# A hybrid stream step: conv sums later, cached keys turned later, values fetched earlier, samples' sums later, and other places for the last tiles

## The chip, the cores and the metric

The kernel runs on one core of one Trainium2 chip. The metric is the device time of one execution in microseconds (us); lower is better. The engines are named as the profile names them: PE (matrix products), PEld (its weight loads), DVE, ACT, POOL (element-wise work), SP (which here issues DMA transfers).

## The reference

One layer of a hybrid trunk, for 512 prompt frames and 64 sample frames (576 together), model width 2048, float32. Half of the input projection feeds eight heads of stick-breaking attention, the other half a gated convolution of three taps over eight channel groups.

```python
hn = rmsnorm(x, g_norm1)
proj = hn @ w_in
q, k, v, gb, gc, hc = split(proj)                 # 3 x 1024 for attention, 3 x 1024 for the conv
q, k = rmsnorm(q), rmsnorm(k)                     # per head
o_attn = stick_breaking_blocks(q, [k_past, k], [v_past, v])
#   z = q k / sqrt(128); A[t,s] = beta_ts * prod_{s<j<t}(1 - beta_tj), s < t
u = gc * hc
o_conv = gb * (conv_w[0]*u[t-2] + conv_w[1]*u[t-1] + conv_w[2]*u[t])
mix = concat([rmsnorm(o_attn), rmsnorm(o_conv)])  # each over its 1024 channels
x = x + mix @ w_out
h2 = rmsnorm(x, g_norm2)
x = x + (silu(h2 @ w_gate) * (h2 @ w_up)) @ w_down
```

Only the sample frames attend to 512 cached keys and values per head. The outputs are x, the new keys and values token by token, and the conv state.

## The kernel before

Activations lie channel by frame: 128 channels on the partitions, 576 frames in two halves of 288. Every operand is split into a rounded high part and the rest (`hi`, `lo`), and three PE products of them make one float32 product.

**Stage A, the input projection,** goes in units of two 128-column blocks; a unit is computed by seven products (n, p_), p_ from 1 to 7, of 24 matmuls each, after Strassen's scheme. The list `order` gives their order. Units have negative numbers, and −2 (queries and keys of the last pair) and −1 (values) are the last. Partial results go from PSUM to SBUF buffers with tags "ms" and "t" (`kept`), copied by ACT at L429. `a_done` finishes a column block c and half i: for queries and keys it scales, squares, and spawns `normed`, which sums squares over channels on PE (`ss`), forms the root on ACT and DVE, and writes the normed tile E (L794). When both halves are there, E is stored to DRAM and `tokens` transposes it into token order (`tok_a`, `tok_b`). E tiles come from the "e" buffers or, for unit −2, from places in `lpool`. `group_scale` sums the squares of the conv output over channels for both halves (`ssg`, in a PSUM bank of the kind `misc`, of which there are two) and writes the conv's scale. The conv's products `mixc` go through DRAM and are loaded back when `xpool` is released after product (−1,3).

**The first half of the output projection** (`out_proj` over `mixc`) is 32 outputs (`pjo`, one of three PSUM banks `ps_pj`) of eight frames with three matmuls each. DVE scales and adds them to x (L1022, L1023). Interleaved with it run the eight heads, `attend(h)`, one begun every 29 frames. In a head, the scores of key blocks 2, 1, 0 (`z`) are followed by the samples' scores against the cached keys (`zs`); then come the running sums and weights of blocks 2, 1, 0 (the matmuls of `weights`), the values (`po`), the samples' running sums (`sample_weights`, L1128 to L1131) and their values. `keys_cached` transposes the 4 blocks of cached keys on PE (`kc`, a bank of `ps_pj`), copies them with ACT (`kcT`) and issues the load of the next head's keys (`cK`). `load_v` loads new and cached values (`vtok`, `cV`) and splits the new ones.

**What sets the order.** A frame of three matmuls is a tick (about 0.40 us here) of a small event queue, `Pipeline`. What is spawned with a delay, or yields a number, comes back after so many ticks and places its PE instructions at that point. PE's order is thus written by hand. The other engines' orders in these stages come from a planner when the program is built. PSUM banks and buffers are handed on by semaphores: whoever takes one waits for its last reader.

The second half of the output projection and the feed-forward network follow.

Of the kernel before, what the change touches and what calls it, by code (L numbers as in the profile page):

```python
# [10 lines left out]
F32 = mybir.dt.float32  # L11
# [90 lines left out]
def tile_hybrid_stream_step(  # L102
# [320 lines left out]
    def run(n, p_, early=False):  # L423
        st = unit[n]
        kind, fp = UNITS[n][:2]

        def kept(tag):
            t = tmp.tile([P, HALF], F32, tag=tag, name="part", bufs=1)
            nc.scalar.copy(out=t, in_=st["y"])  # L429
            return t  # L430

        def done(c, i, ps, part=None):
            if n < 0:
                a_finish(n, c, i, ps, part)
            elif kind != "down":
                finish(kind, fp, c, i, ps, part)
            elif n in last:
                store_y(n, c, i)

        def add(c, i, ps, part=None):  # L440

            if kind != "down":
                return
            if n in first:
                if part is not None:
                    nc.vector.tensor_tensor(out=acc[fp, c, i], in0=ps, in1=part, op=ALU.add)
                else:
                    nc.scalar.copy(out=acc[fp, c, i], in_=ps)
                return
            if ps is not None:  # L450
                nc.vector.tensor_tensor(out=acc[fp, c, i], in0=ps, in1=acc[fp, c, i], op=ALU.add)
            if part is not None:
                nc.gpsimd.tensor_tensor(out=acc[fp, c, i], in0=acc[fp, c, i], in1=part, op=ALU.add)

        if kind == "down" and p_ == 1 and n in first:
            take_blocks(fp)
        later = kind == "down" and n not in first
        if p_ == 1:
            st["y"] = ps_pj.tile([P, HALF], F32, tag="pj", name="psy")
            multiply(st["y"], n, 1, True)  # L460
            st["p1"] = kept("ms")
        elif p_ == 2:
            x = ps_z.tile([P, 512], F32, tag="z0", name="psx2")[:, :HALF]
            multiply(x, n, 2, True)
            add(0, 0, x, st["p1"])
            done(0, 0, x, st["p1"])
        elif p_ == 6:
            multiply(st["y"], n, 6, False)
            st["u2"] = kept("ms" if n == NGU - 1 else "t")
            if later:  # L470
                add(1, 0, None, st["u2"])
        elif p_ == 7:
            st["w"] = ps_z.tile([P, 512], F32, tag=f"z{n % 2 + 1}", name="psw")[:, :HALF]
            multiply(st["w"], n, 7, True)
            if later:
                add(1, 1, st["w"])
            if "u4" in st:
                done(1, 1, st["w"], st["u4"])
        elif p_ == 5:
            multiply(st["y"], n, 5, False)  # L480
            st["u4"] = kept("acc")
            if early:
                done(0, 1, st["v"], st["u4"])
            if "w" in st:
                add(1, 1, None if later else st["w"], st["u4"])
                done(1, 1, st["w"], st["u4"])
        elif p_ == 3 and early:
            st["v"] = ps_pj.tile([P, HALF], F32, tag="pj", name="psv")
            multiply(st["v"], n, 3, True)
        elif p_ == 3:  # L490
            multiply(st["y"], n, 3, False)
            add(0, 1, st["y"])
            done(0, 1, st["y"])
        else:
            multiply(st["w"], n, 4, False)
            add(1, 0, st["w"], None if later else st["u2"])
            done(1, 0, st["w"], st["u2"])
            del unit[n]
# [284 lines left out]
    def normed(n, h, c, a, b, s2, E):  # L783
        yield 12 if n == -2 else 17
        ms = ss = channel_sums(s2[:, 0], s2[:, 1], a, b, "ss")
        yt = hl_tile("yt")
        y, t = yt[:, :HALF], yt[:, HALF:]
        nc.scalar.activation(out=ms, in_=ss, func=AF.Identity, scale=1.0 / P, bias=epsc)
        nc.scalar.activation(out=y, in_=ms, func=AF.Ln)
        nc.scalar.activation(out=y, in_=y, func=AF.Exp, scale=-0.5)  # L790
        nc.scalar.activation(out=t, in_=y, func=AF.Square)
        nc.vector.scalar_tensor_tensor(out=t, in0=t, scalar=-0.5, in1=ms, op0=ALU.mult, op1=ALU.mult)
        nc.vector.scalar_tensor_tensor(out=t, in0=t, scalar=1.5, in1=y, op0=ALU.add, op1=ALU.mult)
        nc.vector.scalar_tensor_tensor(out=E[:, a:b], in0=E[:, a:b], scalar=col("gk") if c else gqs, in1=t,  # L794
                                       op0=ALU.mult, op1=ALU.mult)
        seen[n, c] = seen.get((n, c), 0) + 1
        if seen[n, c] == 2:
            nc.sync.dma_start(out=qk_dram[h, c], in_=E)
            if c:
                pipe.spawn(tokens(E, kp[:, h, :], ks[:, h, :], None, 5 if n == -2 else 20))  # L800

    def group_scale(acc_, bufs):
        for a, b in HALVES:
# [22 lines left out]
    def a_done(n, c, i, ps, part):  # L826
        kind, g = UNITS[n][:2]
        a, b = HALVES[i]
        if kind in ("v", "qk"):
            if (n, c) not in etile:  # L830
                etile[n, c] = lpool.tile([P, UW - 2], F32, tag=f"c{c}", name="E2")[:, :T] if n == -2 else e_tile(f"E{n}")
            E = etile[n, c]
            bank = ps
            if part is not None:
                nc.vector.tensor_tensor(out=E[:, a:b], in0=ps, in1=part, op=ALU.add)
                ps = E[:, a:b]
            nc.vector.tensor_tensor(out=E[:, a:b], in0=ps, in1=R1[:, a:b], op=ALU.mult)
            if kind == "qk":
                sq = hl_tile("sq")[:, :HALF] if c == i == 1 else bank
                s2 = tmp.tile([P, 2, HALF], F32R, tag="hl", name="s2", bufs=3)  # L840
                nc.scalar.activation(out=sq, in_=E[:, a:b], func=AF.Square)
                nc.scalar.copy(out=s2[:, 0], in_=sq)
                nc.vector.tensor_tensor(out=s2[:, 1], in0=sq, in1=s2[:, 0].bitcast(F32), op=ALU.subtract)
                pipe.spawn(normed(n, g, c, a, b, s2, E))
                return
            seen[n, c] = seen.get((n, c), 0) + 1
            if seen[n, c] == 2:
                h = 2 * g + c
                pipe.spawn(tokens(E, vp[:, h, :], vs[:, h, :], v_dram[h], 3 if n == -1 else 7))
            return  # L850
# [73 lines left out]
             (2 - NA, 5)]  # L924
    for n in range(2 - NA, -3):
        order += [(n + 1, 1), (n, 3), (n, 4), (n + 1, 2), (n + 1, 6), (n + 1, 7), (n + 1, 5)]
    order += [(-2, 1), (-3, 3), (-3, 4), (-2, 2), (-2, 6), (-1, 1), (-2, 5), (-1, 2), (-2, 3), (-2, 7), (-1, 3),
              (-1, 6), (-2, 4), (-1, 5), (-1, 7), (-1, 4)]
    early = {-NA, 1 - NA, -1}
    mixc = []  # L930
# [2 lines left out]
    for k_, (n, p_) in enumerate(order):  # L933
        run(n, p_, n in early)
        if k_ + 4 < len(order):
            prepare(*order[k_ + 4])
            if order[k_ + 4] in ((-2, 3), (-1, 6)):
                load_weight()
        if (n, p_) == (-2, 6):
            pipe.spawn(group_scale(accc[0], 3), 5)  # L940
        if (n, p_) == (-1, 3):
            xpool.release()
            cpool = tc.alloc_tile_pool(name="cpool", bufs=1, reuse_waits="tile", side="right")
            mixc = cpool.tile([P, NG, 2, T], F32R, name="mixc")
            for g in range(NG):
                nc.sync.dma_start(out=mixc[:, g].bitcast(F32), in_=mixc_dram[g])
        if (n, p_) == (-1, 7):
            split_weight(nc.vector)
# [26 lines left out]
    def load_cached_keys(h):  # L975
        nc.sync.dma_start(out=cK, in_=ck[:, h, :].rearrange("(i p) d -> p i d", p=P))

    load_qk(0)
    load_cached_keys(0)
    nc.vector.tensor_scalar(out=neg1r, in0=ident, scalar1=0.0, scalar2=-1.0, op0=ALU.mult, op1=ALU.add)  # L980
    onef = oner.bitcast(F32)
    neg1f = neg1r.bitcast(F32)
# [62 lines left out]
    def open_b():  # L1045
# [6 lines left out]
        v_ = v_.rearrange("p (f i d) -> p f i d", f=2, d=P)  # L1052
        bt["vh"], bt["vl"] = ([v_[:, f, 0], v_[:, f, 1], vz[:, f]] for f in range(2))
        bt["v2"] = v_
        load_v(0)

    def load_v(h):
        nc.sync.dma_start(out=vtok, in_=v_dram[h])
        nc.sync.dma_start(out=cV, in_=cv[:, h, :].rearrange("(i p) d -> p i d", p=P))
        split(bt["v2"][:, 0], bt["v2"][:, 1], vtok[:, 0:2, :])  # L1060
        split(bt["vh"][2], bt["vl"][2], vtok[:, 2, :])

# [11 lines left out]
    def attend(h):  # L1074
# [46 lines left out]
            nc.gpsimd.tensor_tensor(out=sums[:, b * TS : (b + 1) * TS], in0=sums[:, (b + 1) * TS : (b + 2) * TS],  # L1121
                                    in1=sp[:, (b + 1) * TS : (b + 2) * TS], op=ALU.add)
        yield 8
        if h + 1 < NH:
            keys_cached(h + 1)

        def sample_weights():
            mm(zs[:, :320], trir, sph[:, :320], stop=False, **kw)  # L1128
# [25 lines left out]
        behind = weights(1)  # L1154
        with tc.issue_after(behind):
            split(sph, spl, sp)
        yield 4
        mm(zb[0], trir, ph[0], stop=False, **kw)
        mm(zb[0], trir, pl[0], stop=False, **kw)
        mm(zb[0][:, P:], neg1r, s0h, stop=False, **kw)  # L1160
# [15 lines left out]
        for i in (2, 1, 0):  # L1176
            for n, (a_, b_) in enumerate(((vh, ph), (vl, ph), (vh, pl))):
                mm(po[:, i * P : 512], a_[i], b_[i][:, : 512 - i * P], stop=(i == 0 and n == 2), **kw)
            if i == 2:
                yield 1  # L1180
                sample_weights()
                yield 2
            elif i == 1:
                yield 3
        mixed(po, 0, TP)
# [12 lines left out]
            else:  # L1198
                nc.gpsimd.tensor_tensor(out=accA[:, a:b], in0=accA[:, a:b], in1=sq[q], op=ALU.add)
        if h + 1 < NH:  # L1200
            load_v(h + 1)

    PERIOD = 29

# [404 lines left out]
```

## Time and profile before

| | |
|---|---|
| median of 3 runs | 2394.09 us (2393.43 to 2395.15) |
| the profiled execution | 2397.15 us, span 2395.4 us |
| granted PE clock, mean | 0.995 |
| busy share PE, DVE, ACT, POOL | 98%, 81%, 52%, 13% |

The span runs from the first to the last instruction of the profiled execution; its time includes what lies around them. In a timeline, a row is a group of like instructions that follow one another: start, length, engine, line, operation, output and inputs, forms, count, and in brackets the idle time ahead of it with what ended it. Ends of matmuls are modelled.

### The profile page before, as it was taken

What the parts mean: (1) busy time and instruction counts of PE and PEld (TensorE: products, weight loads), DVE (VectorE), ACT (ScalarE), POOL (GpSimd) and SP (SyncE); (2) the same over time, 40 slices, a digit from 0 to 9 for tenths busy, and PEclk for the clock granted to TensorE, in tenths of its full rate; (3) what the DMA queues carried; (4) which work ended last, traced back from release to release, by engine and by line L of the source; (5) the groups of instructions that cost most, each with busy time, mean ns of one, the idle gap of its engine ahead of it and who ended that gap; (6) DMA issues with size and microseconds to landing.
All of it is one profiled execution on the core that took longest, in us unless ns stands there. A gap on an engine that the chain in (4) does not pass through costs nothing.

```text
span 2395.4 us, 43789 instructions
## 1 busy us (share of the span) xinstructions
PE 2350.2 (98%) x17609; PEld 2336.2 (98%) x17609; DVE 1934.0 (81%) x2828; ACT 1234.6 (52%) x2211; POOL 300.3 (13%) x377
## 2 busy tenths in 40 slices
PE   8899999999999999999999999999999899999998
PEld 8899999999899999999999999999999899999998
DVE  7888888787677768888888888888888768887875
ACT  7456656455777545444444444444444444444454
POOL 0111121120233221000000000000000002431211
PEclk9999999999999999999999999999999999999999
DMA  7433343525733333444444444345354936875642
GB/s 254 141 113 104 114 138 89 162 88 188 236 105 104 107 135 106 141 150 132 139 151 142 129 150 153 118 156 159 109 157 139 338 111 212 225 222 194 204 129 79
DMA packets 474900, 360.60 MB, mean 151 GB/s; under 512 B 11278, under 2 KB 460680, under 8 KB 474696
## 3 DMA queue, kind: packets, MB, share of 16 engines
q1 hardware_dynamic: 469528, 351.02, 45.8%
q0 software_dynamic: 5168, 6.79, 1.6%
q8 instruction: 138, 2.26, 0.4%
q14 instruction: 66, 0.54, 0.1%
HBM read 281.39 MB, written 76.37 MB: 149 GB/s over the span
## 4 chain that ended last, share of the span: by engine, by line
PE 82%; DVE 6%; ACT 4%; issue 2%; DMA 1%; POOL 1%; SPq 0%; DVEq 0%; ACTq 0%; POOLq 0%
PE psy L406 43%; PE psw L406 21%; PE psx L406 10%; PE pjo L227 5%; DVE whl L232 1%; DMA v_dram<-tok 1%; PE pw L1391 1%; ACT whl L231 1%; ACT ph L231 0%; PE pot L1514 0%; DVE c L881 0%; ACT whi L179 0%; DMA raw_a<-in_w_down_dram 0%; DVE raw_b L350 0%; DVE wlo L180 0%
## 5 line engine op out<-in xcount | busy, mean ns | idle before, releaser
L232 DVE TENSOR_TENSOR whl<-raw_a,whl 128x1024 fp32r<-128x1024 f32 (+4 forms) x376 | 424.6, 1130 | 70.2 <-ACT whl L231 68.5
L406 PE MATMUL psy<-t,whl 128*128 128x288 f32 x2916 | 437.3, 295 | 0.5 <-ACT part L429 0.5
L231 ACT CAST whl<-raw_a 128x1024 fp32r<-128x1024 f32 (+4 forms) x376 | 352.3, 938 | 141.4 <-PE psx L406 52.1
L406 PE MATMUL psy<-h_s,whl 128*128 128x288 f32 x2724 | 411.8, 295 | 6.8 <-ACT part L429 6.8
L406 PEld LDWEIGHTS psy<-t,whl 128*128 128x128 f32 x2916 | 403.4, 189 | 0.9 <-ACT part L429 0.7
L406 PEld LDWEIGHTS psy<-h_s,whl 128*128 128x128 f32 x2724 | 378.7, 189 | 7.3 <-ACT part L429 7.3
L406 PE MATMUL psw<-t,whl 128*128 128x288 f32 x2592 | 377.2, 295 | 0.0
L406 PEld LDWEIGHTS psw<-t,whl 128*128 128x128 f32 x2592 | 354.0, 189 | 0.2
L232 DVE TENSOR_TENSOR whl<-raw_b,whl 128x1024 fp32r<-128x1024 f32 (+5 forms) x230 | 247.7, 1077 | 89.3 <-ACT whl L231 87.8
L231 ACT CAST whl<-raw_b 128x1024 fp32r<-128x1024 f32 (+5 forms) x230 | 207.2, 903 | 208.2 <-PE psw L406 70.0
L429 ACT COPY part<-psy 128x288 f32<-128x288 f32 x303 | 120.8, 399 | 350.0 <-PE psy L406 345.4
L406 PE MATMUL psx<-h_s,whl 128*128 128x288 f32 x1122 | 166.8, 297 | 2.7 <-DVE gs L1371 2.7
L406 PEld LDWEIGHTS psx<-h_s,whl 128*128 128x128 f32 x1122 | 156.2, 191 | 2.9 <-issue 2.9
L231 ACT CAST whl<-s 128x1024 fp32r<-128x1024 f32 (+5 forms) x101 | 93.3, 924 | 119.9 <-PE psw L406 114.1
L406 PE MATMUL psy<-t12a,whl 128*128 128x288 f32 x1056 | 150.0, 295 | 2.0 <-ACT part L429 2.0
L406 PE MATMUL psw<-t34a,whl 128*128 128x288 f32 x1056 | 150.4, 295 | 1.4 <-DVE ghs L869 0.9
L406 PEld LDWEIGHTS psy<-t12a,whl 128*128 128x128 f32 x1056 | 143.2, 188 | 2.7 <-ACT part L429 2.7
L406 PEld LDWEIGHTS psw<-t34a,whl 128*128 128x128 f32 x1056 | 143.4, 188 | 1.9 <-DVE ghs L869 1.1
L232 DVE TENSOR_TENSOR whl<-s,whl 128x1024 fp32r<-128x1024 f32 (+5 forms) x101 | 107.5, 1065 | 19.9 <-ACT whl L231 18.1
L227 PE MATMUL pjo<-mixc,whi 128*128 128x288 f32 x512 | 119.4, 300 | 0.0
L1334 POOL DMA_DIRECT2D hid_dram<-form x3 | 2.4, 807 | 923.9 <-DVE form L232 923.9
L227 PE MATMUL pjo<-mixa,whi 128*128 128x288 f32 x512 | 102.7, 295 | 0.0
(599 smaller groups left out, 4138.4 us busy)
## 6 DMA issues: line engine op xcount, KB each, us to landing
hid_dram<-form SPq DMA_DIRECT2D x147, 288.0 KB, 2.3
raw_a<-in_w_gate_dram SPq DMA_DIRECT2D x23, 1024.0 KB, 6.4
raw_a<-in_w_up_dram SPq DMA_DIRECT2D x23, 1024.0 KB, 6.0
raw_a<-in_w_in_dram SPq DMA_DIRECT2D x22, 1024.0 KB, 5.5
raw_b<-in_w_in_dram SPq DMA_DIRECT2D x22, 1024.0 KB, 8.2
raw_b<-in_w_gate_dram SPq DMA_DIRECT2D x21, 1024.0 KB, 6.7
raw_b<-in_w_up_dram SPq DMA_DIRECT2D x21, 1024.0 KB, 7.8
h_s<-hid_dram SPq DMA_DIRECT2D x10, 2016.0 KB, 9.9
```

The source lines that it names most:

```text
L227: mm(ps, w_[:, k, csl], x_[:, a:b], start=(k == 0 and n == 0), stop=(k == nk - 1 and n == 2))
L231: cast = nc.scalar.copy(out=hi, in_=src)
L232: (lo_eng or nc.vector).tensor_tensor(out=lo, in0=src, in1=hi.bitcast(F32), op=ALU.subtract)
L406: mm(ps, whl[:, w_, j, :], x_, start=(start and j == 0 and q == 0), stop=(j == len(xs_) - 1 and q == 2), skip_group_check=True)
L429: nc.scalar.copy(out=t, in_=st["y"])
L1334: q.dma_start(out=hid_dram[fp][2 * n - 2 : 2 * n].rearrange("f p t -> p f t"), in_=t.bitcast(F32))
L1391: mm(pss[j, i], w_[:, k, j * P : (j + 1) * P], x_, start=(kk == 0 and k == 0 and n == 0), stop=(kk == 1 and k == 7 and n == 2))
```

## The change

Eight edits, all between about 552 us and the end of the first half of the output projection:

1. `u2` of unit −1 is kept in the buffer "ms" rather than "t".
2. The tokens of unit −2's keys lag 11 ticks rather than 5 behind their norm.
3. Of units −2 and −1 the tiles with c = 0 lie in `lpool`, those with c = 1 in "e" buffers. Before, both of −2 were in `lpool` and both of −1 in "e".
4. Product (−1,3) comes ahead of (−2,7); with it the release of `xpool` and the `mixc` loads.
5. `group_scale` starts 13 ticks after (−2,6) rather than 5.
6. The values of head 0 (`fetch_v`) are requested behind the first queries and keys, and split at tick 15 of head 0; later heads as before.
7. `keys_cached(h + 1)` moves from tick 15 to tick 24 of a head, two ticks behind the second block's weights.
8. `sample_weights` moves from tick 29 to tick 31 of a head.

```diff
-            st["u2"] = kept("ms" if n == NGU - 1 else "t")
+            st["u2"] = kept("ms" if n in (-1, NGU - 1) else "t")
...
-                pipe.spawn(tokens(E, kp[:, h, :], ks[:, h, :], None, 5 if n == -2 else 20))
+                pipe.spawn(tokens(E, kp[:, h, :], ks[:, h, :], None, 11 if n == -2 else 20))
...
-                etile[n, c] = lpool.tile([P, UW - 2], F32, tag=f"c{c}", name="E2")[:, :T] if n == -2 else e_tile(f"E{n}")
+                etile[n, c] = (lpool.tile([P, UW - 2], F32, tag=f"c{n + 2}", name="E2")[:, :T]
+                               if n > -3 and c == 0 else e_tile(f"E{n}"))
...
-    order += [(-2, 1), (-3, 3), (-3, 4), (-2, 2), (-2, 6), (-1, 1), (-2, 5), (-1, 2), (-2, 3), (-2, 7), (-1, 3),
+    order += [(-2, 1), (-3, 3), (-3, 4), (-2, 2), (-2, 6), (-1, 1), (-2, 5), (-1, 2), (-2, 3), (-1, 3), (-2, 7),
               (-1, 6), (-2, 4), (-1, 5), (-1, 7), (-1, 4)]
...
-            pipe.spawn(group_scale(accc[0], 3), 5)
+            pipe.spawn(group_scale(accc[0], 3), 13)
...
+    def fetch_v(h):
+        nc.sync.dma_start(out=vtok, in_=v_dram[h])
+        nc.sync.dma_start(out=cV, in_=cv[:, h, :].rearrange("(i p) d -> p i d", p=P))
+
     load_qk(0)
     load_cached_keys(0)
+    fetch_v(0)
...
-        load_v(0)
-
-    def load_v(h):
-        nc.sync.dma_start(out=vtok, in_=v_dram[h])
-        nc.sync.dma_start(out=cV, in_=cv[:, h, :].rearrange("(i p) d -> p i d", p=P))
+
+    def split_v():
         split(bt["v2"][:, 0], bt["v2"][:, 1], vtok[:, 0:2, :])
         split(bt["vh"][2], bt["vl"][2], vtok[:, 2, :])
...
         yield 8
-        if h + 1 < NH:
-            keys_cached(h + 1)
+        if h == 0:
+            split_v()
...
-        yield 4
+        yield 2
+        if h + 1 < NH:
+            keys_cached(h + 1)
+        yield 2
         mm(zb[0], trir, ph[0], stop=False, **kw)
...
             if i == 2:
-                yield 1
+                yield 3
                 sample_weights()
-                yield 2
...
         if h + 1 < NH:
-            load_v(h + 1)
+            fetch_v(h + 1)
+            split_v()
```

## The prediction

> **What bounds the kernel now.** I read the page's head, then busy time by stage, then the waits of the tensor engine in the stretch that the change touches, then the timelines of single engines around those waits.
>
> ```profile
> span 2395.4 us, 43789 instructions
> PE 2350.2 (98%) x17609; PEld 2336.2 (98%) x17609; DVE 1934.0 (81%) x2828; ACT 1234.6 (52%) x2211; POOL 300.3 (13%) x377
> 520.00:600.00 80.00, 75.34 (x562) 74.23 (x561) 60.78 (x86) 43.61 (x78) 10.29 (x12) 1.00 0.49 162
> 600.00:784.00 184.00, 177.00 (x1284) 170.68 (x1283) 135.90 (x290) 139.01 (x315) 58.28 (x105) 1.00 0.44 145
> 950.00:1840.00 890.00, 888.99 (x6700) 888.79 (x6701) 747.04 (x1020) 412.40 (x619) 0.79 (x1) 1.00 0.45 141
> ```
>
> The first two lines are the page's; the others are windows (from:to, length, busy PE, PEld, DVE, ACT, POOL, granted clock, DMA share, GB/s). PE is busy 98% of the span at full clock, and no matmul is taken away. So the change can gain only PE's idle time in its own stretch, from the last units of the input projection (about 552 us) to the end of the first half of the output projection (784 us): 80.0 − 75.3 = 4.7 us and 184.0 − 177.0 = 7.0 us, some 11.7 us in all. The long feed-forward stage from 950 us loses 1 us of 890; it starts earlier by what is gained ahead of it and hands nothing back. Which idle time it is, the waits of PE between 540 and 790 us say (total, times, longest):
>
> ```profile
> PE kc L1066 <- DMA cK<-in_cache_k_dram: 2.5, 1, 2.5
> PE zs L1129 <- DVE spl L232: 2.3, 6, 0.6
> PE ssg L805 <- DVE yt L792: 2.2, 1, 2.2
> PE z L1150 <- ACT ph L231: 1.1, 1, 1.1
> PE psy L406 <- ACT part L429: 1.0, 1, 1.0
> PE tok_a L759 <- DVE neg1r L980: 0.9, 1, 0.9
> PE zs L1128 <- ACT sph L231: 0.6, 1, 0.6
> PE psw L406 <- DVE E-1_6622 L835: 0.6, 1, 0.6
> PE po L1178 <- ACT hbe L231: 0.2, 1, 0.2
> ```
>
> Each wait costs a little more than is shown, for idle time counts from the modelled end of the matmul before:
>
> ```profile
> 575.17 2.14 PE L406 MATMUL psv<-bod,whl 128*128 128x288 f32 x15
> 572.00 3.33 PE L406 MATMUL psw<-t34a,whl 128*128 128x288 f32 x24
> 582.08 3.33 PE L406 MATMUL psw<-t34a,whl 128*128 128x288 f32 x24
> 586.39 3.48 PE L406 MATMUL psy<-t12a,whl 128*128 128x288 f32 x24 [0.98 <-ACT part L429]
> ```
>
> Undisturbed, a group of 24 is followed by the next after 575.17 − 572.00 = 3.17 us, though 3.33 is shown as its length; at 582.08 the next comes after 4.31 us, so that wait cost 1.14, not 0.98. I add 0.16 us for each wait. A "tick" below is three matmuls of 3.17/24 = 0.132 us, 0.40 us.
>
> **Conv sums eight ticks on.** The second half's `ssg` waits for the reader of the first half's PSUM bank.
>
> ```profile
> 561.09 0.75 PE L805 MATMUL ssg<-accc,oner 128*128 128x288 f32 x2 [2.19 <-DVE yt L792]
> 560.59 0.45 DVE L792 SCALAR_TENSOR_TENSOR yt<-yt,ss 128x288 f32<-128x288 f32 x1
> ```
>
> The built order puts the two `ssg` behind the norm sums `ss` with both banks of that kind read out, so 2.2 goes. The first use of the conv scale is some 40 us later; nothing becomes late.
>
> **The copy `u2` of unit −1 in another buffer.** Product (−1,5) stands still (586.39 above) until ACT has copied (−1,6), whose buffer unit −2 still holds. With the "ms" buffer the copy follows its own product, a whole product (3.17 us) before it is needed: 1.0 goes.
>
> **Tokens lag 5 to 11, tile swap.** The transposes of unit −2's keys come too early for their norm chain:
>
> ```profile
> 592.13 0.29 PE L286 MATMUL ss<-s,oner 128*128 128x288 f32 x1
> 595.75 0.52 DVE L794 SCALAR_TENSOR_TENSOR E<-E,vec,yt 128x288 f32<-128x288 f32 x1
> 596.41 0.63 PE L759 MATMUL tok_a<-ident,E 128*128 128x128 f32 x4 [0.93 <-DVE neg1r L980]
> ```
>
> From `ss` to the finished tile it is 595.75 + 0.52 − 592.13 = 4.1 us. Lag 5 asks for it earlier, and six more ticks (2.4 us) put the transposes behind it: 0.9 goes. The tile that is read last now lies outside the pool whose space the heads' buffers reuse:
>
> ```profile
> 599.71 0.58 SPq L970 DMA_DIRECT2D qf<-qk_dram  x1
> ```
>
> The first query load is issued at 599.71, behind everything of this stage; by the built order it stands ahead of the stores of the last tiles on SP, so it comes earlier by about what the stage gains, which pays for the earlier start of the heads. The exchange of (−1,3) and (−2,7) brings the eight loads of `mixc` one product (3.17 us) forward; I cost it at nothing, as they stay covered by later products. The 0.6 at `psw` stays. Stage A: 2.2 + 1.0 + 0.9 = 4.1, with three times 0.16, 4.6 us.
>
> **Cached keys turned at tick 24, first values fetched with the queries.**
>
> ```profile
> 613.83 0.38 SPq L976 DMA_DIRECT2D cK<-in_cache_k_dram  x1
> 617.17 0.63 PE L1066 MATMUL kc<-ident,cK 128*128 128x128 f32 x4 [2.54 <-DMA cK<-in_cache_k_dram]
> 628.33 0.41 PE L1128 MATMUL zs<-sph,trir 128*128 128x320 f32 x1 [0.57 <-ACT sph L231]
> 629.22 0.41 PE L1129 MATMUL zs<-spl,trir 128*128 128x320 f32 x1 [0.47 <-DVE spl L232]
> ```
>
> Head 1's cached keys are issued at 613.83 and awaited at 617.17. The transposes move nine ticks on, 9 × 0.40 = 3.6 us; that exceeds the 2.5 awaited even without the attention matmuls between, so it goes. With them goes the next `cK` load, which has a whole head until its own use. The first `vtok` and `cV` loads leave the place behind the token stores on SP for one ahead of the first two `x` loads, and delay those by their bytes; I take that as paid for by the earlier issue above. `split_v` in head 0 uses what landed long before. The early block wait at `z` (1.1) I leave as it is, for `ph` is neither nearer nor farther: a weight cast comes ahead of it on ACT, and the keys' copy leaves.
>
> **Samples' sums two ticks on.** `sample_weights` now stands 0.8 us and four score matmuls (about 0.5 us) later, 1.3 us. All its waits (0.6 once; six of up to 0.6) are shorter, so 0.6 + 2.3 goes; the 0.2 at `po` lies in the same chain. What follows it, `ws` for the heads' last matmuls, is 1.3 us later and was earlier than needed by more than that.
>
> Removed in all: 2.2 + 1.0 + 0.9 + 2.5 + 0.6 + 2.3 + 0.2 = 9.7 shown, in 3 + 1 + 1 + 6 + 1 = 12 waits, plus 12 × 0.16 = 1.9: **11.6 us**.
>
> **What is added.** Turned at tick 24, the keys take one of the three banks that `pjo` and `po` also use, right ahead of `po`. By the built order `po` gets the keys' bank in heads 2 and 5 and then waits for ACT's copy `kcT`, which stands in ACT's queue behind other work:
>
> ```profile
> 668.43 0.67 ACT L231 CAST sph<-hbl 128x576 fp32r<-128x576 f32 x1
> 664.11 0.58 ACT L1067 COPY kcT<-kc 128x512 f32<-128x512 f32 x1
> 669.08 0.38 PE L1175 MATMUL po<-pr,vtok 128*128 128x128 f32 x2
> 732.12 0.48 ACT L1140 ACTIVATE hbl<-z 128x384 f32<-128x384 f32 x1
> 734.61 0.62 ACT L231 CAST ph<-pr 128x512 fp32r<-128x512 f32 x1
> 732.40 0.38 PE L1175 MATMUL po<-pr,vtok 128*128 128x128 f32 x2
> 707.99 0.43 PE L227 MATMUL pjo<-mixc,whi 128*128 128x288 f32 x2
> 708.79 0.45 DVE L1023 TENSOR_TENSOR x<-pjo,x 128x288 f32<-128x288 f32 x1
> ```
>
> Head 2: behind `sph`, 669.10 + 0.58 = 669.68 against `po` at 669.08, 0.6. Head 5: behind the exponential, 732.60 + 0.58 = 733.18 against 732.40, 0.8. In head 4 a `pjo` group, due at 708.12 (the second matmul of that row), takes over a bank that DVE leaves at 709.24: 1.1. For the copy of head 0 against its `zs` I put 0.1. With 0.16 for three waits, 0.6 + 0.8 + 1.1 + 0.1 + 0.5 = **3.1 us**. Bounds: nothing, if the engines run ahead there; at most about 6 us, with one cast more ahead of the copy in head 2 (0.6 + 0.6, as long as the cast at 734.61) and two more in head 5 (0.8 + 1.2), the 1.1, and 1.0 for the first copy (the `z` wait of head 0 is the nearest), plus 0.16 each. I take 3.1, since it follows from the queue order that the program has.
>
> **Rivals.** *The copy in the queue.* That a ready copy waits on ACT is seen already:
>
> ```profile
> 724.75 0.60 PE L1066 MATMUL kc<-ident,cK 128*128 128x128 f32 x4
> 728.27 0.57 ACT L1067 COPY kcT<-kc 128x512 f32<-128x512 f32 x1
> ```
>
> The keys were ready at 725.35 and copied at 728.27, 2.9 us later. At tick 15 nobody needed the bank; at tick 24 `po` may. The Trainium skill, "Perfetto Trace Analysis", section "Tensor Engine Instruction (MATMUL, LD_WEIGHTS)", says that ACT, DVE and GpSimd work through their queues strictly in order and that only PE can reorder, by pulling weight loads ahead; the trace agrees, as the 2.9 us at 725 show, and the rule speaks against putting a bank's release into this queue late in a head. If the copy stood behind the last exponential's cast in all seven turns (734.61 + 0.62 + 0.58 = 735.81 against 732.40), each would cost 3.4 + 0.16 = 3.6, 25 in all, and 25 − 11.6 = 13.4 us slower, 2407.5. From 11.6/7 = 1.7 us a turn it eats the gain. Against it: the built order gives `po` that bank twice only, and behind less. Chance 0.06.
>
> *The loads stay late.*
>
> ```profile
> 610.00:620.00 10.00, 7.46 (x60) 7.26 (x59) 3.85 (x9) 5.77 (x14) 0.92 (x2) 1.00 1.03 348
> 620.00:630.00 10.00, 7.72 (x51) 6.69 (x50) 8.90 (x20) 8.38 (x18) 3.66 (x7) 1.00 0.98 368
> ```
>
> In these windows the DMA share is 1. If the DMA is what starts the heads, the same bytes land no sooner, and head 0's waits (2.5 + 0.6 + 0.5 with 0.5 for the three) come back as others. What remains is 11.6 − 4.1 − 3.1 = 4.4 us, 2389.7. Against it: keys awaited 3.6 us later need no faster DMA. Chance 0.13.
>
> *Nothing happens*, because each wait that goes is followed by another on the same chain, as the second `zs` wait follows the first: 2394. Chance 0.03.
>
> **The numbers.** 11.6 − 3.1 = 8.5 us. The profiled execution, 2397.15 with a span of 2395.4, would come to 2388.65 and 2386.9; it lies 3.1 above the median of the runs, from which I forecast 2394.09 − 8.5 = **2385.6 us** (chance 0.78). The low end is the gain without a new wait, 2382.5; the high end takes in 6 us of new waits (2388.5) and the late loads with 0.8 us of stage A lost besides, 2390.5. What a measurement of this kernel can tell from no change is about 0.2%, 4.8 us: faster 0.80 (the forecast and a little of the second rival), same 0.14, slower 0.06.
>
> **What would show it.** In the changed profile: no wait at `ssg`, at `psy` of (−1,5) or at the second `tok_a`, and the first `pjo` about 4.6 us before 599.38 (stage A right); no wait of `kc` for `cK`, and `zs` without waits (heads right); new waits of `po` for `kcT` of under 1 us in heads 2 and 5 and one of a `pjo` for DVE. The forecast is wrong if the first `pjo` is early but the end of the first half is not, or if `po` waits for `kcT` in most heads.

## The result and the profile after

| | before | changed |
|---|---|---|
| median of 6 runs | 2394.62 us (2393.43 to 2398.77) | 2384.86 us (2381.42 to 2386.16) |
| profiled execution, span | 2397.15 us, 2395.4 us | 2384.66 us, 2383.0 us |

The ratio of the runs is 0.9954, 95% interval 0.9945 to 0.9964. The medians differ by 9.8 us; 8.5 were forecast. The head of the changed kernel's page:

```profile
span 2383.0 us, 43801 instructions
PE 2345.5 (98%) x17609; PEld 2333.6 (98%) x17609; DVE 1934.5 (81%) x2828; ACT 1234.1 (52%) x2211; POOL 298.5 (13%) x377
```

The waits of PE in the changed stretch (total, times, longest), to be held against the nine of before (a tenth, 0.2 us at `z` for DVE's `pl`, is not shown there):

```profile
PE pjo L227 <- DVE x L1029: 1.5, 1, 1.5
PE po L1181 <- ACT kcT L1070: 1.0, 1, 1.0
PE z L1153 <- ACT ph L231: 0.7, 1, 0.7
PE psw L406 <- DVE E-1_6622 L836: 0.6, 1, 0.6
PE z L1154 <- DVE pl L232: 0.4, 1, 0.4
PE kc L1069 <- DVE x L1029: 0.2, 1, 0.2
```

The waits at `ssg`, `psy`, `tok_a`, of the first `kc` for its load and at all `zs` are gone; two new ones, for a bank, stand on top, and a third of 0.2 us stands last. Where the time came from is read best from three starts on PE's timeline: the first matmul of product (−2,6), the first `pjo`, and the first matmul of the output projection's second half. Before:

```profile
552.44 3.33 PE L406 MATMUL psy<-t12a,whl 128*128 128x288 f32 x24
...
599.38 0.30 PE L227 MATMUL pjo<-mixc,whi 128*128 128x288 f32 x1
...
783.96 0.29 PE L227 MATMUL pjo<-mixa,whi 128*128 128x288 f32 x1
```

Changed:

```profile
553.45 3.33 PE L406 MATMUL psy<-t12a,whl 128*128 128x288 f32 x24
...
595.38 0.38 PE L227 MATMUL pjo<-mixc,whi 128*128 128x288 f32 x1
...
775.41 0.29 PE L227 MATMUL pjo<-mixa,whi 128*128 128x288 f32 x1
```

I call the two distances A (stage A) and B (heads). A goes from 46.94 to 41.93, 5.0 us shorter; B from 184.58 to 180.03, 4.55 shorter; together 9.6. What lies behind the second half (102.6 us in both) differs by 3.9 us in this pair of executions; 2.8 of them are a stretch at half clock, told at the end of the experiments, and I do not count them as the change's.

### The profile page after: what moved, and what is told of

The parts are those of the page before. It is cut to its first block, busy times and chain, and to the rows that moved or that the text cites. A ratio compares the mean times of both kernels' runs of the same rounds, so it can differ in the third digit from the quotient of the medians.

```text
span 2383.0 us, 43801 instructions
## 1 busy us (share of the span) xinstructions
PE 2345.5 (98%) x17609; PEld 2333.6 (98%) x17609; DVE 1934.5 (81%) x2828; ACT 1234.1 (52%) x2211; POOL 298.5 (13%) x377
## 4 chain that ended last, share of the span: by engine, by line
PE 85%; DVE 5%; ACT 3%; issue 2%; POOL 1%; DMA 1%; SPq 0%; DVEq 0%; ACTq 0%; POOLq 0%
PE psy L406 44%; PE psw L406 22%; PE psx L406 10%; PE pjo L227 5%; DVE whl L232 1%; PE pw L1397 1%; ACT ph L231 0%; PE psv L406 0%; PE pot L1520 0%; DVE c L882 0%; DMA x<-xt_dram 0%; ACT whl L231 0%; DVE raw_b L350 0%; PE tok_a L759 0%; POOL ta L1318 0%
```

## The experiments

Each distance is read as above, in one profile of each kernel. Between the two profiles of the changed kernel A differs by less than 0.1 us and B by 0.5. Each time was taken beside the kernel before, whose median lay between 2393.4 and 2395.1 us. The last column says for how long within A and B the granted PE clock stood at 0.50 instead of 1.00.

| kernel | A | B | time, us (runs) | clock at 0.50, us |
|---|---|---|---|---|
| before | 46.9 | 184.6 | 2394.6 (6) | none |
| changed | 41.9 | 180.0 | 2384.9 (6) | none |
| edits 1 to 5 alone | 41.9 | 184.0 | 2389.6 (11) | none |
| edits 6 to 8 alone | 47.0 | 183.5 | 2395.0 (11) | 3.4 in B |
| edit 7 alone | 46.9 | 188.9 | 2396.4 (1) | twice 3.4 in B |
| edit 8 alone | 48.5 | 186.3 | 2399.7 (1) | 3.4 in A, 6.8 in B |
| changed, edit 3 undone | 41.9 | 185.8 | 2389.2 (8) | 6.8 in B |
| changed, edit 6 undone | 41.9 | 185.7 | 2391.9 (1) | 3.4 in B |
| changed, edit 7 undone | 41.9 | 185.2 | 2389.2 (1) | none |
| changed, edit 8 undone | 41.9 | 183.8 | 2388.7 (1) | none |
| changed, edit 7 in head 0 only | 41.9 | 182.2 | 2385.3 (5) | 3.4 in B |
| changed, keys of head 2's turn at tick 22 | 41.9 | 179.7 | 2383.1 (5) | none |
| changed, once more | 41.9 | 180.5 | 2383.5 (5) | none |

In six kernels, then, B holds a stretch at half clock, each begun during a wait of PE or within 2 us behind one. These are windows that lie within the stretches, in the order of the table (two each for edit 7 alone; the column before the last two is the granted clock):

```profile
620.60:624.00 3.40, 3.40 (x15) 3.25 (x14) 2.75 (x6) 3.10 (x8) 2.62 (x5) 0.50 0.56 174
617.50:620.80 3.30, 3.04 (x13) 2.69 (x12) 2.58 (x7) 2.46 (x6) 0.28 (x1) 0.50 1.01 312
624.30:627.60 3.30, 3.30 (x16) 3.29 (x15) 3.30 (x6) 2.88 (x8) 3.00 (x6) 0.50 0.13 50
620.60:627.40 6.80, 5.06 (x23) 5.09 (x24) 2.79 (x7) 4.82 (x11) 1.23 (x2) 0.50 1.02 317
602.90:609.60 6.70, 6.28 (x24) 5.99 (x25) 2.35 (x6) 2.77 (x7) 0.87 (x2) 0.50 1.03 357
617.80:621.10 3.30, 3.30 (x16) 3.28 (x15) 3.30 (x7) 2.90 (x7) 3.00 (x6) 0.50 0.32 123
719.40:722.70 3.30, 3.30 (x13) 3.30 (x14) 1.96 (x7) 1.72 (x4) 1.51 (x5) 0.50 0.00 0
```

From the end of the wait to the end of the stretch, the matmuls took longer than the same matmuls in a kernel that runs them at full clock: by 1.6 us (edits 6 to 8), 2.9 (edit 7, both stretches), 2.3 (edit 8), about 3 (edit 3 undone), 1.6 (edit 6 undone) and 1.5 (edit 7 in head 0 only). B less this loss is given below as an estimate of B at full clock; it is one because a PE that comes later can also find a later wait shorter.

**Edits 1 to 5 alone.** The first five hunks of the diff, the heads as before.

> The kernel before with the edits 1 to 5 alone (stage A). Two stretches on the tensor engine are read: A from the first matmul of (-2,6) to the first pjo (46.9 us before, 41.9 changed), B from there to the first matmul of the second half (184.6 before, 180.0 changed). Theory (each wait is the tensor engine's own, and the parts add up): A 41.9, B 184.6, time about 5 us below before. Rival (the heads are started by the DMA): A 41.9, but head 0's waits grow by what stage A gained, B 187 to 189, time 0 to 2 us below before.

A 41.9 and B 184.0, ratio to before 0.9978 (0.9969 to 0.9987), 5.5 us by the medians. The theory holds: stage A's waits were PE's own, and the heads do not give the gain back. Edits 1, 2, 4 and 5 were not run apart; that three of them took a wait each is read from the rows, and of edit 4, which was priced at nothing, no run shows the share.

**Edits 6 to 8 alone.** The other hunks, stage A as before.

> The kernel before with the edits 6 to 8 alone (heads). Theory: A stays 46.9, B about 180, time some 4.6 us below before. Rival (the gain of head 0 comes from the loads that the tile swap lets start earlier, and the values' loads ahead of x cost): A 46.9, B 183 or more, time at most 1.5 us below before, with head 0's first add of x waiting longer than 2.0 us.

B 183.5 and a ratio of 0.9998 (0.9989 to 1.0007): nothing in the time. The parts do not add up (5.5 and 0.1 us against 9.8), so the theory fell in its second half. In B, 1.6 us are half clock; at full clock it would be about 181.9, which is 2.7 below before instead of 1.1, and with the 0.6 of edits 1 to 5 makes 3.3 of the 4.55. Why the times show none of this is open; one of the 11 executions has a profile. The longer waits of PE in the heads of this kernel:

```profile
PE po L1179 <- ACT kcT L1069: 1.6, 1, 1.6
PE pjo L227 <- DVE x L1028: 1.5, 1, 1.5
PE z L1151 <- ACT ph L231: 1.4, 1, 1.4
PE kc L1068 <- DVE x L1028: 0.4, 2, 0.2
```

The waits for `cK` and at `zs` have gone here too, yet the block wait at `z` (1.4 against 0.7) and the bank wait of `po` (1.6 against 1.0) are longer than with stage A's edits. The rival's effect is there: the first query load is issued 0.5 us behind the first `pjo` (598.77 against 598.24), in the changed kernel 2.6 us ahead of it. Its other sign, a longer wait of DVE for x, was not seen, and its 183 was met only with the half clock.

**Edit 7 alone.**

```diff
         yield 8
-        if h + 1 < NH:
-            keys_cached(h + 1)
...
-        yield 4
+        yield 2
+        if h + 1 < NH:
+            keys_cached(h + 1)
+        yield 2
```

> The kernel before with edit 7 alone (cached keys at tick 24). Theory: the wait of 2.7 for the first keys goes and bank waits of po and pjo of about 4 us in all come in the heads 2, 4, 5 and 6, so B is 185 to 186: by itself the edit costs about 1 us, and its gain lies in head 0 only. Rival (turning late is the gain of the heads): B 182 or less.

B 188.9: 4.3 us longer than before, dearer than either expected. But 2.9 of that are the two stretches at half clock; what is left, about 186.0, is what the theory expected for B, though with waits at `z` in head 0 that it did not have. The wait for `cK` is gone, but these stand in its place (PE, then ACT):

```profile
PE z L1147 <- ACT ph L231: 2.5, 1, 2.5
PE po L1175 <- ACT kcT L1067: 2.4, 2, 1.6
PE z L1143 <- ACT hbe L231: 1.4, 1, 1.4
```

```profile
ACT hbe L231 <- DMA vtok<-v_dram: 2.9, 1, 2.9
```

The 2.5 us that PE had spent waiting for the keys had covered another lateness: the cast of the first values waits 2.9 us for its load (1.8 before), and the blocks' casts stand behind it on ACT. With PE no longer held, it arrives early at `z`. The cast itself also starts 1.4 us later, counted from the first `pjo` (17.55 against 16.19); why its load lands later is open.

**Edit 8 alone.**

```diff
-                yield 1
+                yield 3
                 sample_weights()
-                yield 2
```

> The kernel before with edit 8 alone (samples' sums two ticks later). Theory: no wait at the zs lines, B 180 to 181 (0.6 and 2.3 us shown, and some 0.2 to 0.5 us more for each of the seven from start to start). Rival (the next step on the same chain takes the wait over, the samples' weights or values): zs waits gone, new waits at the os matmuls or at po, B 183 or more.

B 186.3; less 2.3 us of half clock behind the wait of `kc`, about 184.0, which is 0.6 below before. The `zs` waits shrink to 0.3, and the time comes back elsewhere, though not at the places that the rival named first:

```profile
PE kc L1066 <- DMA cK<-in_cache_k_dram: 3.9, 1, 3.9
PE pjo L227 <- ACT kcT L1067: 2.3, 1, 2.3
PE po L1175 <- ACT pr L1140: 0.8, 1, 0.8
```

The wait of `pjo` for `kcT` appears in the three kernels that have late sums with keys at tick 15 in later heads (this one, edit 7 undone, edit 7 in head 0 only), 2.3 us each time, and in no other with more than 0.2. A's 48.5 is another matter, told below.

**Edit 7 in head 0 only.**

```diff
+        if 0 < h < NH - 1:
+            keys_cached(h + 1)
...
-        if h + 1 < NH:
+        if h == 0:
             keys_cached(h + 1)
```

The first place is tick 15, the second tick 24.

> The changed kernel, but the cached keys are turned at tick 24 in head 0 alone, in heads 1 to 6 at tick 15 as before. Theory (late turning is needed only where the load of the second head's keys is late, and later it costs a bank that po and pjo wait for): the waits of po for kcT and of pjo for DVE's add go (1.2 + 1.8 + 0.8 from start to start), B about 176.5 against 180.0, time some 3 us below the changed kernel. Rival (at tick 15 the copies take ACT's time ahead of the weights, and the block waits come back, as when the sums were moved alone): B 180 or more.

B 182.2, 2.2 us longer than in the changed kernel; time ratio to before 0.996 (0.9946 to 0.9974). The theory, which had 176.5, fell: the bank waits did go, and those of the early turn came instead.

```profile
PE pjo L227 <- ACT kcT L1070: 2.3, 1, 2.3
PE po L1183 <- ACT pr L1145: 0.8, 1, 0.8
```

Of the 2.2 us, 1.5 are the half clock behind this wait of `pjo`. The 0.7 that is left is close to the 0.5 between the two profiles of the changed kernel, and the times do not tell the two kernels apart. So the early turn gains nothing in the later heads; that the late turn gains there is not shown.

**Edit 7 undone.** Keys at tick 15 in all heads.

> The changed kernel with edit 7 undone (keys turned at tick 15 in every head). Theory: the wait of kc for the load of cK is back with 2 to 4 us in head 0, no bank waits in the heads 2 to 6; B 179 to 181, about as with the edit: over the eight heads edit 7 gains little. Rival (edit 7 is what carries the heads' gain): B 184 or more.

B 185.2, all at full clock: 5.2 us lost, so the rival was right in this. `kc` waits 2.0 us for `cK` again, `pjo` 2.3 us for `kcT`, and some `zs` and `po` waits of 0.2 to 0.8 return.

**Edit 3 undone.** Tiles of unit −2 both in the pool that the heads reuse.

> The changed kernel with edit 3 undone (both tiles of unit -2 in the pool that the heads' buffers reuse). Theory (the heads' edits gain only because the swap lets the first loads start some 4 us earlier against the end of stage A): A stays near 42, the first query load is issued behind the first pjo again, and B rises from 180.0 to about 183.5, as with the heads' edits alone; time about 3 us above the changed kernel. Rival (the swap is worth nothing by itself, the parts merely fit together in the order that the planner finds): B 180.

A 41.9, B 185.8, ratio to before 0.9977 (0.9967 to 0.9987). The swap is worth nothing to stage A and 5.8 us to the heads, more than was expected; about 3 of the 5.8 are the half clock behind the wait below, and the rest is what the theory had. The runs show the loss as well: their ratio of 0.9977 lies outside the interval of the changed kernel, 0.9945 to 0.9964. PE's longest wait in this kernel, its first query load, and its first `pjo`:

```profile
PE z L1087 <- ACT kh L231: 2.4, 1, 2.4
```

```profile
596.47 0.50 SPq L970 DMA_DIRECT2D qf<-qk_dram  x1
```

```profile
595.05 0.38 PE L227 MATMUL pjo<-mixc,whi 128*128 128x288 f32 x1
```

The query load is issued 1.4 us behind the first `pjo`; in the changed kernel it is 2.6 us ahead of it (592.73 against 595.38). The first scores now wait 2.4 us for the keys' cast.

**Edit 6 undone.** Values requested when the heads open.

> The changed kernel with edit 6 undone (first values requested and split when the heads open, behind the token stores). Theory (late turning and early values belong together: with late values the cast of vtok stands in front of the weights on ACT): the block waits z of head 0, 1.6 us from start to start now, rise to 3 or more as with edit 7 alone; B 182 to 184. Rival (values are hidden anyway): B 180.

B 185.7, or about 184.1 without the half clock. As with edit 7 alone, the cast of `vtok` waits for its load (1.9 us on ACT) and PE for the blocks behind it:

```profile
PE z L1148 <- ACT ph L231: 3.3, 1, 3.3
```

**Edit 8 undone.** Sums at tick 29.

> The changed kernel with edit 8 undone (samples' sums at tick 29 again). Theory (the sums' waits are real and end with the edit): waits at the zs lines return in head 0 and in the later heads, 3 to 5 us in all from start to start, and B rises from 180.0 to 183 to 185, as it did when any one of the other three was undone. Rival (with the keys turned late ACT is free earlier, and the sums no longer wait): no zs waits, B 180 to 181.

B 183.8, all at full clock. The `zs` waits return with 0.4 and 1.1 us shown, and the waits of `po` for `kcT` grow to 2.5 in two heads.

**Head 2's turn at tick 22.**

```diff
-        yield 2
+        lead = {2: 0}.get(h, 2)
+        yield lead
         if h + 1 < NH:
             keys_cached(h + 1)
-        yield 2
+        yield 4 - lead
```

> The changed kernel with the keys of head 2's turn at tick 22 rather than 24, where they stand ahead of two casts on ACT; all other turns at 24. Theory (the new po wait is the copy behind those casts): the 1.2 us at head 2's po goes, nothing else moves, B 178.9; time about 1 us below the changed kernel, too little to be told by times alone. Rival (the copy ahead of the casts delays the weights): the wait comes back at the next matmuls of that head, B 180.

The `po` wait is gone, as foreseen, but B is 179.7, not 178.9: two thirds of the 1.2 us came back, 0.25 at a `pjo` that waits for `kcT` and 0.5 at a `kc` (a wait of 0.7 in place of 0.2). With 2383.1 against 2383.5 us beside it, the times do not tell the two kernels apart.

**The changed kernel once more.**

> The changed kernel once more, beside the last. A 41.9 and B 180.0 again within 0.1. Theory of the clock (the half clock behind the 2.7 us wait at the start of the feed-forward stage falls in some executions of either kernel): the stretch from the last pjo to the last matmul lies anywhere from 1498.5 to 1502.4 us, as it did in the runs so far whatever was changed ahead of it. Rival (the change itself spares the half clock): 1498.5 again.

A 41.9, B 180.5, ratio to before 0.9955 (0.9943 to 0.9968): the result stands. B is 0.5 longer than in the first profile, more than the 0.1 that was expected; 0.3 of it lies in head 0, whose cached scores wait for the copy `kcT` here. The stretch behind the last `pjo` took 1499.4 us here; in the first pair it was 1498.5 (changed) and 1502.4 (before). No half clock stands at the start of its feed-forward stage either.

**The clock behind the 2.7 us wait.** In the profile of before, the product behind the wait at the start of the feed-forward stage ran at half speed; in the changed one it did not. Windows of before, then of the changed kernel (the column before the last two is the granted clock):

```profile
950.00:956.00 6.00, 5.48 (x23) 5.51 (x24) 5.03 (x7) 2.12 (x4) 0.79 (x1) 0.50 0.33 115
956.00:960.00 4.00, 4.00 (x30) 4.00 (x30) 2.72 (x4) 1.14 (x2) 0.00 (x0) 0.93 0.00 0
```

```profile
942.00:945.00 3.00, 3.00 (x23) 3.00 (x24) 3.00 (x4) 2.08 (x4) 0.41 (x1) 1.00 0.31 107
```

The same product in the kernels with edit 6 undone and with edit 8 undone, whose wait began at the same time (946.15 − 2.90 = 943.25 and 945.93 − 2.67 = 943.26 us):

```profile
946.15 5.38 PE L406 MATMUL psx<-h_s,whl 128*128 128x288 f32 x21 [2.90 <-DVE gs L1371]
```

```profile
945.93 3.05 PE L406 MATMUL psx<-h_s,whl 128*128 128x288 f32 x21 [2.67 <-DVE gs L1377]
```

One ran 21 matmuls in 5.4 us, the other in 3.05, with nearly the same idle time ahead, and the program of that stage is the same in both.

The traces tell what differs. In each of them the starts and ends of the stretches at half clock lie whole multiples of 3.413 us apart; with edit 8 alone, for example, they run from 562.55 to 565.97, 620.58 to 627.41 and 955.09 to 958.50, and from the first of these times to the last are 116 steps. Cut every trace into steps of this length, counted from there, and take the steps from 80 to 2370 us that run at full clock: in the 13 traces half clock follows each step in which PE was busy for at most 0.41 of the time and none in which it was busy for 0.57 or more; between 0.44 and 0.56 both occur. The steps around the wait are, with edit 6 undone and then with edit 8 undone:

```profile
941.97:945.39 3.42, 1.28 (x10) 1.05 (x8) 3.39 (x5) 2.33 (x3) 0.00 (x0) 1.00 0.34 123
```

```profile
941.16:944.57 3.41, 2.10 (x16) 1.86 (x15) 3.38 (x4) 2.51 (x4) 0.00 (x0) 1.00 0.24 87
944.57:947.99 3.42, 2.06 (x15) 2.09 (x16) 3.42 (x6) 1.90 (x5) 0.80 (x1) 1.00 0.51 180
```

In the first most of the wait falls into one step, which leaves PE busy for 1.28 of 3.42 us; in the second it is split between two, with 2.10 and 2.06 us busy. The Trainium skill, "TensorE: Matmul & The Clock Gate", section "Part 1: The HAM clock gate", says that the clock is set by activity in a window of about 3.4 us that runs freely, not from the kernel's start; the steps of 3.413 us agree with that. So the 2.8 us of this product hang on where the wait falls in these steps, and I do not count them as a gain of the change. Five of the thirteen profiles miss the half clock here: the two of the changed kernel, edit 8 undone, head 2's turn moved, and edit 7 alone, which has stage A as before. Four kernels that share most of the changed kernel's edits show it. Whether the changed kernel is spared more often isn't settled. The kernel with edit 8 alone shows the same gate in stage A, behind the 2.2 us wait at `ssg`:

```profile
563.00:565.00 2.00, 2.00 (x9) 1.85 (x8) 1.02 (x3) 0.89 (x2) 0.00 (x0) 0.50 1.05 367
```

That is its A of 48.5: not the edit, but a wait that at times costs some 1.5 us more than its length. The edit on the conv's sums takes away this risk too.

## Why the prediction was right, and where its steps were not

**Stage A** was forecast with 4.6 us and gave 5.0. All three waits went as described:

```profile
562.07 0.65 PE L805 MATMUL ssg<-accc,oner 128*128 128x288 f32 x2
...
562.95 0.65 PE L805 MATMUL ssg<-accc,oner 128*128 128x288 f32 x2
```

```profile
595.02 0.60 PE L759 MATMUL tok_a<-ident,E-2_6461 128*128 128x128 f32 x4
```

No idle time stands ahead of either. The 0.4 us beyond the forecast lie in gaps of 0.1 to 0.2 us at the matmuls next to the old waits.

**The heads** were forecast with 11.6 − 4.6 − 3.1 = 3.9 us and gave 4.55. The waits for `cK` and at all `zs` went, and head 0's wait at `z` stayed (1.1 + 0.2 before, 0.7 + 0.4 after). The new waits came at the forecast places and with the forecast cause, somewhat dearer:

```profile
660.65 0.67 ACT L231 CAST sph<-hbl 128x576 fp32r<-128x576 f32 x1
661.23 0.58 ACT L1070 COPY kcT<-kc 128x512 f32<-128x512 f32 x1
```

```profile
661.86 0.49 PE L1181 MATMUL po<-pr,vtok 128*128 128x128 f32 x2 [1.01 <-ACT kcT L1070]
...
702.42 0.40 PE L227 MATMUL pjo<-mixc,whi 128*128 128x288 f32 x1 [1.52 <-DVE x L1029]
```

Head 2's `po` starts when `kcT`, behind `sph`, has ended (661.81): 1.0 shown for 0.6 forecast. Head 4's `pjo` waits 1.5 for 1.1. Head 5's `po`, forecast with 0.8, shows no idle time, and a wait of 0.2 at a `kc` was not forecast. So 2.7 us are shown for the 2.6 forecast; that three terms, each off by 0.4 or more, cancel so well is luck. In the queue, the copy held `po` once, not seven times, so the first rival did not come about; nor did the second.

**The step that failed** is one that the sum does not show: it priced the edits one by one, by the wait that each removes. By that, edit 7 is worth about nothing (2.5 removed, with 0.16, and 3.1 added), edit 6 is put at nothing, and the swap of the tiles merely pays for the earlier start. The runs show another thing. Taken back from the whole, edit 7 costs 5.2 us in B, edit 8 3.8, edit 6 5.7 (about 4.1 at full clock) and edit 3 5.8 (about 3). Taken alone, edit 7 makes B 4.3 us longer and edit 8 1.7 (at full clock about 1.4 longer and 0.6 shorter), and the three without stage A's edits gain 1.1 (about 2.7), and nothing in the time; edit 6 was not run alone. So edits 7 and 8 are worth more with the others than without them. The swap also did more than pay: the first query load went from 599.71 to 592.73, 7.0 us earlier where about what the stage gains was forecast, and from 0.3 us behind the first `pjo` to 2.6 ahead of it. The sum was right because it was made for the whole change by the order that the whole program has; used for a part, the same reasoning missed by 4 to 6 us with edit 7 undone, by about 4 with edit 7 in head 0 only and by 3 to 4 with edit 8 alone, the half clock taken off. The third rival's mechanism (each wait that goes is followed by another on the same chain) is what edits 7 and 8 show when they stand alone; for the edits taken together it did not come about.

## What to carry to other kernels

A wait on the busiest engine also hides what is late behind it: before pricing its removal, ask which operand of the next steps lands during that wait, and move that too, as the first values' load had to be moved here. Edits that share a chain (load, cast, bank, matmul) are to be priced and tried together; by their times, edit 7 alone, edit 8 alone and the three of the heads without stage A's would have been thrown away. A distance between two rows of one engine's timeline tells a difference of over 0.5 us where the whole time, with 1 to 7 us between runs, does not; but first the granted clock of the two stretches is to be compared, which here was worth 1.5 to 3 us in six of them.

## What was not expected of the hardware

A wait of PE of 1.4 to 3.9 us was followed in many of these traces by 3.4 or 6.8 us at a granted clock of 0.50, which made the matmuls behind it 1.3 to about 3 us later still. In other executions such a wait is followed by full clock: with edit 7 in head 0 only the wait of `pjo` for `kcT`, 2.28 us, has the half clock behind it, and with edit 7 undone the same wait, 2.31 us, has not. This makes part of the spread of the times, and a single profile's span mixes it into the comparison: 12.4 us between the two spans here, of which 9.6 are the change's.
